# A macaron decoder block on one core: where the down stage's operands are combined, split and kept

## The chip, the cores and the metric

The kernel runs on one core of a Trainium2 chip. The metric is the time of one execution on the device, in microseconds; three runs of the kernel before the change stand at 2628.35, 2628.57 and 2629.67 us. The engines are TensorE (PE in the profile; PEld are its weight loads), VectorE (DVE), ScalarE (ACT) and GpSimd (POOL); SyncE (SP) issues most of the DMA transfers. Each engine works through its own instructions in order.

## The reference

The block is a half-step SwiGLU, a token mixer, a second half-step SwiGLU and a final RMS norm, on 1024 tokens of width 1024. The change touches only the two SwiGLU halves:

```python
D_MODEL, SEQ, D_FF = 1024, 1024, 2816

def swiglu(h, w_gate, w_up, w_down):
    return (jax.nn.silu(h @ w_gate) * (h @ w_up)) @ w_down

h = h + 0.5 * swiglu(rms_norm(h, ffn1_norm), ffn1_w_gate, ffn1_w_up, ffn1_w_down)
h = h + hybrid_mixer(rms_norm(h, mix_norm), ...)
h = h + 0.5 * swiglu(rms_norm(h, ffn2_norm), ffn2_w_gate, ffn2_w_up, ffn2_w_down)
return rms_norm(h, final_norm)
```

All of it is float32. The kernel reaches that precision with three matmuls for one: every operand x is split into hi (a cast to fp32r) and lo (x minus hi), and hi*lo, lo*hi and hi*hi are added up in PSUM.

## The kernel before, in words

Everything is kept transposed: 128 features on the partitions, 1024 tokens in the free dimension. D_FF is 22 tiles of 128 features, numbered j = 0 to 21.

**Gate/up stage** (`ffn`, `gate_up2`, `strassen`). Tiles 0 and 1 are made plainly, the others in pairs (j, j + 1), ten pairs in a half block. A pair is one Strassen run for the gate and one for up, each of seven products (`product`, twelve matmuls each, line 368) over sums of activation tiles that lie ready in SBUF (`t2`, `t3`, `t4` and `xs`). The weights come as four quarters a11, a12, a21, a22 in tiles `raw` (two buffers) and `sr` (two buffers); POOL makes the four sums of them that Strassen needs (`combine`, line 356), ACT casts the hi part (line 126) and DVE subtracts the lo part (line 127) for each product. ACT copies finished products out of PSUM (`keep`, line 374: c11 after the first product, c21 after the third, c22 after the fourth), DVE adds others to them (`add`, line 379). The third product is accumulated into the same PSUM bank as the first, after c11 is copied. The results of a pair are two tiles `s` of 1024 tokens, in halves: b11, b12 (the first tile), b21, b22 (the second). `put_gate` and `put_up` make silu(gate) * up in them; the last half to be ready is b12, from the seventh product of the up run. Both tiles of the pair are then stored to DRAM in float32 (`a_d`, line 490).

**Down stage.** First block D0 (tiles 18 and 19): `accumulate` with plain matmuls (line 139), update of h by DVE (line 282). Then four chunks of four tiles each (DCH), each a Strassen scheme over two parts (k = 0, 1) of two tiles: the part's seven operands b11, b21, t2, t3, t1, t4, b22 are made from its two tiles by four sums on POOL (lines 510, 511, 517 and 520, in `part_steps`) and seven splits (ACT line 126, DVE line 127). A chunk runs four groups g of seven products (`down`, line 575; 168 matmuls), each group with its weights loaded, summed on POOL (lines 586 to 589) and split; DVE adds each product into h (`put`, line 580). While a chunk runs, `prepare` loads the four float32 tiles of the next chunk from `a_d` (SP, line 548) and its operands are made, a step behind each weight split (`advance`). Chunk 0's first part is the pair just made (20, 21); its second part and the operands of its first part are made beside D0. The operands of even chunks lie in the tiles `t2h` to `t4l` and four smaller ones, those of odd chunks in the tiles that held the gate/up activations. The tail (tiles 12 to 15) is loaded and split at the end of the last chunk and runs with plain matmuls.

**What sets the order.** A scheduler of the framework sorts the instructions of each engine; what stands under `tc.high_priority` (weight splits, `keep`, `add`, `put`) goes ahead of its place in the program, and `tc.issue_after` holds an instruction behind a named one. On the chip an engine does not pass over an instruction that waits.

Of the kernel before, what the change touches and what calls it, by code (L numbers as in the profile page):

```python
# [7 lines left out]
F32 = mybir.dt.float32  # L8
F32R = mybir.dt.float32r
# [6 lines left out]
P = 128  # L16
T = 1024
# [3 lines left out]
NF = FF // P  # L21
# [2 lines left out]
NCH = T // P  # L24
QSQ = (EPS * P) ** 0.5
D0 = [18, 19]
DCH = [[20, 16, 21, 17], [0, 2, 1, 3], [4, 6, 5, 7], [8, 10, 9, 11]]
DTAIL = [12, 13, 14, 15]
HALVES = ((0, 512), (512, 512))
LO, HI = slice(0, 512), slice(512, 1024)  # L30
FIRST = ((0, 256), (256, 256), (512, 512))
# [17 lines left out]
def tile_macaron_hybrid(  # L49
# [123 lines left out]
    def run(steps):  # L173
        while True:
            try:
                next(steps)
            except StopIteration as e:
                return e.value
# [110 lines left out]
                for (ui, _, _), n in zip(units, ("t3h", "t3l", "t4h", "t4l"))]  # L289

    def s_tile(tp):
        return tp.tile([P, T], F32, name="s", tag="s", bufs=2)

    def norm_space(tp):
        w = [t[:, i * 512:i * 512 + 512] for t in (s_tile(tp), s_tile(tp)) for i in range(2)]
# [129 lines left out]
    def ffn(h, xs, wg, wu, wd, tq, tp, ysc, first, last, pre, steps, after):  # L425
        def act_tiles():
            return [tq.tile([P, T], F32R, name=n, tag=n, bufs=2) for n in ("ah", "al")]
# [20 lines left out]
            nc.sync.dma_start(out=a_d[j], in_=a)  # L448

        done = []  # L450
        a_d = dram.tile([NF, P, T], F32, name="a_d")

        def stage():
            return tp.tile([P, 512], F32, name="sr", tag="sr", bufs=2)
# [10 lines left out]
        def gate_up2(j):  # L465
            ss = [s_tile(tp), s_tile(tp)]

            def put_gate(i, sl, c, _):
                s, y = ss[i][:, sl], ysc[:, sl]
                with tc.high_priority(offset=400):  # L470
                    nc.vector.tensor_mul(out=s, in0=y, in1=c)
                    nc.scalar.activation(out=s, in_=s, func=AF.Silu)  # L472
                    nc.gpsimd.tensor_mul(out=s, in0=s, in1=y)  # L473

            strassen(wg[j], wg[j + 1], put_gate)
            hs = []

            def put_up(i, sl, c, _):
                s = ss[i][:, sl]
                with tc.high_priority(offset=400):  # L480
                    nc.vector.tensor_mul(out=s, in0=s, in1=c)
                    if j == D0[0]:
                        if not hs:
                            hs.extend(zip(act_tiles(), act_tiles()))
                        split(s, hs[0][i][:, sl], hs[1][i][:, sl])

            strassen(wu[j], wu[j + 1], put_up)
            if j < D0[0]:
                for i in (1, 0):
                    nc.sync.dma_start(out=a_d[j + i], in_=ss[i])  # L490
            return list(zip(*hs)) if hs else ss

        def part_steps(k, ss, ops):
            (b11, b12), (b21, b22) = ([t[:, LO], t[:, HI]] for t in ss)
# [30 lines left out]

        def chunk_ops(c):
            names = ("b11", "b21", "t2", "t3", "t1", "t4", "b22")
            res = {}
            for i, n in enumerate(names):
                if c % 2:  # L530
                    res[n] = [[t[:, k] for k in range(2)] for t in
                              (xn.tile([P, 2, 512], F32R, name=f"x{p}{i}", tag=f"x{p}{i}") for p in "hl")]
                elif i < 6:
                    m = ("t2h", "t2l", "t3h", "t3l", "t4h", "t4l")[i]
                    t = tq.tile([P, 4, 512], F32R, name=m, tag=m)
                    res[n] = [[t[:, 2 * p + k] for k in range(2)] for p in range(2)]
                else:
                    res[n] = [[tp.tile([P, 512], F32R, name=m, tag=m, bufs=bf) for m, bf in q]
                              for q in ((("c11", 1), ("c21", 1)), (("c22", 1), ("wt", 2)))]
            return res  # L540

        def prepare(c, ops, first=None):
            parts = [first] if first else []
            for k in range(len(parts), 2):
                ss = [p.tile([P, T], F32, name=n, tag=n, bufs=2)
                      for p, n in (((tq, "ah"), (tq, "al")) if k and c else ((tp, "s"), (tp, "s")))]
                for i in range(2):
                    nc.sync.dma_start(out=ss[i], in_=a_d[DCH[c][2 * i + k]])
                parts.append(ss)
            for k in range(2):  # L550
                yield from part_steps(k, parts[k], ops)
# [67 lines left out]
            gate_up2(j)  # L619
        acts = gate_up2(D0[0])  # L620
        ss = gate_up2(NF - 2)
        ops = chunk_ops(0)
        prep = prepare(0, ops, ss)
        advance(prep, None)
        accumulate(wd, block_units([D0])[0], acts, h, 0.5, step=lambda i: advance(prep, None))
        run(prep)
        for c in range(len(DCH)):
            prep = None
            if c + 1 < len(DCH):
                nops = chunk_ops(c + 1)  # L630
                prep = prepare(c + 1, nops)
                advance(prep, None)
            for g in range(4):
                down(wd[2 + 4 * c + g], ops, h[2 * g], h[2 * g + 1], prep)
            if prep:
                run(prep)
            ops = nops
        acts = []
        kept = []
        for n in ("t2h", "t2l"):  # L640
            t = tq.tile([P, 4, 512], F32R, name=n, tag=n).rearrange("p (j a) t -> p j (a t)", j=2)
            kept.append([t[:, k] for k in range(2)])
        for i, j in enumerate(DTAIL):
            t = s_tile(tp)
            nc.sync.dma_start(out=t, in_=a_d[j])
            acts.append([x[i] for x in kept] if i < 2 else act_tiles())
            split(t, *acts[-1])
        tail = [(2 + 4 * len(DCH) + i, 2 * i, 2) for i in range(4)]
        prev = (tail, acts)
        sqrt_table()  # L650
# [13 lines left out]
    with ExitStack() as st:  # L664
        tq = pool(st, "q1")
        hp = pool(st, "h1")
        tp = pool(st, "t1")
# [39 lines left out]
    with ExitStack() as st:  # L707
        with ExitStack() as stm:
            ys, h, tq = mixer(stm, st, tc, pool, start, xs2, load_unit, dense, ptile, bank, rsqrt_newton, split, new_x,
                           accumulate, block_units(OBLOCKS), dram, pr, ident, ones, cst, eye, wlr, win,  # L710
                           wout, y_d, h_d, sqrt_table, strassen_products, rp, psum, divide, recent, pinned, run)
        tp = pool(st, "t2")
# [10 lines left out]
        res = []  # L723
# [735 lines left out]
```

## Time and profile before

| | us |
|---|---|
| median of three runs | 2628.57 |
| the profiled execution, as a run | 2629.9 |
| its span in the trace | 2628.1 |
| gate/up stage, one pair | 38.08 |
| D0, first and second half block | 28.60, 26.89 |
| chunks 0 to 2 together, first and second half block | 134.31, 135.90 |
| chunk 3, first and second half block | 38.25, 38.80 |

The profile has one execution. Its span is the time from the first to the last instruction; the run's own time is a little longer. Stages are cut at the start of the first matmul that belongs to them. In a table of windows, the first number behind a stretch is its length, then follow the busy times of the engines with the number of instructions that begin in it, the clock granted to TensorE as a share of full speed, the busy share of the 16 DMA engines and the rate. A matmul's row gives its duration in the pipeline; consecutive matmuls start closer together than that.

### The profile page before, as it was taken

To read this page: it belongs to the slowest core of one execution; us is meant where nothing else is said; L and a number is where in the kernel's file an instruction comes from. 1 tells how busy PE (TensorE), PEld (TensorE's weight loads), DVE (VectorE), ACT (ScalarE), POOL (GpSimd) and SP (SyncE) were. 2 spreads that over 40 slices of the span, in tenths; PEclk is the share of its full clock that TensorE was granted. 3 is DMA by queue.
4 is the path that set the end of the run, shared out by engine and by line. 5 is a ranking of instruction groups with operands and counts; after the bars stand their busy time and mean duration, and the time that the engine had idled before them with its cause. 6 is when DMAs were issued, how large, how long until landed. Compare 5 with 4: busy or idle time off the path is not lost.

```text
span 2628.1 us, 32714 instructions
## 1 busy us (share of the span) xinstructions
PE 2490.9 (95%) x11656; PEld 2018.1 (77%) x11656; DVE 1877.5 (71%) x2907; ACT 1069.3 (41%) x1847; POOL 1175.8 (45%) x1312
## 2 busy tenths in 40 slices
PE   7899999899997999999989999999989999998998
PEld 6788888677866877777767787877868888886677
DVE  8855555899686778886686766767586555569996
ACT  5333334333252444443354544535243333343331
POOL 4554444654228667776351222122044444446631
PEclk9999999999998999999989999999989999999999
DMA  3222221322321222212211212113212222223222
GB/s 118 75 70 88 89 89 57 120 81 80 113 84 49 65 61 61 65 45 57 57 55 40 85 38 84 60 61 128 85 33 81 84 77 85 89 60 114 79 88 80
DMA packets 93602, 199.03 MB, mean 76 GB/s; under 512 B 12248, under 2 KB 17112, under 8 KB 93440
## 3 DMA queue, kind: packets, MB, share of 16 engines
q1 hardware_dynamic: 82576, 175.64, 20.6%
q0 software_dynamic: 8704, 18.89, 2.8%
q10 hardware_dynamic: 2160, 2.43, 0.3%
q8 instruction: 91, 1.49, 0.2%
q14 instruction: 71, 0.58, 0.1%
HBM read 158.73 MB, written 38.17 MB: 75 GB/s over the span
## 4 chain that ended last, share of the span: by engine, by line
PE 69%; DVE 14%; ACT 5%; issue 4%; POOL 3%; DMA 2%; DVEq 0%; POOLq 0%; ACTq 0%
PE q L368 28%; PE ps L139 15%; PE m L368 10%; PE q L575 6%; DVE wl L127 3%; PE q L989 2%; DVE h L580 1%; DVE xl L127 1%; DVE ha L580 1%; PE q L911 1%; DMA s<-a_d 1%; ACT L806 1%; PE q L1002 1%; PE q L1026 1%; POOL xp L936 1%
## 5 line engine op out<-in xcount | busy, mean ns | idle before, releaser
L127 DVE TENSOR_TENSOR wl<-raw,wh 128x512 fp32r<-128x512 f32 x244 | 209.3, 858 | 167.3 <-ACT wh L126 165.9
L139 PE MATMUL ps<-xl,wh 128*128 128x512 f32 (+2 forms) x736 | 257.1, 408 | 18.2 <-DVE xl L239 13.3
L127 DVE TENSOR_TENSOR wl<-sr,wh 128x512 fp32r<-128x512 f32 x232 | 204.0, 880 | 80.5 <-ACT wh L126 80.2
L139 PE MATMUL ps<-xh,wl 128*128 128x512 f32 (+2 forms) x736 | 254.4, 404 | 0.1
L139 PE MATMUL ps<-xh,wh 128*128 128x512 f32 (+2 forms) x736 | 254.0, 405 | 0.0
L368 PE MATMUL q<-xl,wh 128*128 128x512 f32 x640 | 249.0, 389 | 0.5 <-ACT c L374 0.5
L368 PE MATMUL q<-xh,wh 128*128 128x512 f32 x640 | 249.0, 389 | 0.0
L368 PE MATMUL q<-xh,wl 128*128 128x512 f32 x640 | 249.0, 389 | 0.0
L126 ACT CAST wh<-sr 128x512 fp32r<-128x512 f32 x232 | 143.8, 620 | 244.0 <-PE q L368 59.8
L473 POOL TENSOR_TENSOR s<-s,ysc 128x512 f32<-128x512 f32 x80 | 112.4, 1416 | 244.0 <-ACT s L472 244.0
L126 ACT CAST wh<-raw 128x512 fp32r<-128x512 f32 x244 | 144.7, 593 | 173.1 <-PE q L368 95.4
L139 PEld LDWEIGHTS ps<-xl,wh 128*128 128x128 f32 (+1 forms) x736 | 138.1, 192 | 49.5 <-DVE xl L239 8.7
L356 POOL TENSOR_TENSOR raw<-sr 128x512 f32<-128x512 f32 x20 | 27.3, 1367 | 331.3 <-DMA sr<-in_win 234.4
L139 PEld LDWEIGHTS ps<-xh,wl 128*128 128x128 f32 (+1 forms) x736 | 139.0, 192 | 24.2 <-issue 1.0
L139 PEld LDWEIGHTS ps<-xh,wh 128*128 128x128 f32 (+1 forms) x736 | 138.0, 192 | 24.5 <-issue 1.0
L368 PEld LDWEIGHTS q<-xl,wh 128*128 128x128 f32 x640 | 120.1, 188 | 25.8 <-issue 0.9
L368 PEld LDWEIGHTS q<-xh,wh 128*128 128x128 f32 x640 | 120.1, 188 | 25.0
L368 PEld LDWEIGHTS q<-xh,wl 128*128 128x128 f32 x640 | 120.1, 188 | 24.9
L379 DVE TENSOR_TENSOR c<-c,q 128x512 f32<-128x512 f32 x120 | 82.4, 687 | 74.6 <-PE q L368 74.5
L374 ACT COPY c<-q 128x512 f32<-128x512 f32 x120 | 70.6, 588 | 152.8 <-PE q L368 151.0
L933 POOL TENSOR_TENSOR itmp<-lt,xp 128x112 f32<-128x112 f32 (+29 forms) x248 | 114.6, 462 | 36.7 <-DMA lt<-l_d 17.9
L936 POOL TENSOR_TENSOR xp<-xp,itmp 128x112 f32<-128x112 f32 (+29 forms) x248 | 118.9, 480 | 19.4
(490 smaller groups left out, 6833.5 us busy)
## 6 DMA issues: line engine op xcount, KB each, us to landing
sr<-in_win SPq DMA_DIRECT2D x80, 256.0 KB, 2.6
a_d<-s SPq DMA_DIRECT2D x36, 512.0 KB, 3.7
raw<-in_win SPq DMA_DIRECT2D x66, 256.0 KB, 2.6
raw<-in_d SPq DMA_DIRECT2D x56, 256.0 KB, 2.6
raw<-in_g SPq DMA_DIRECT2D x48, 256.0 KB, 2.6
s<-a_d SPq DMA_DIRECT2D x24, 512.0 KB, 4.3
sr<-in_u SPq DMA_DIRECT2D x44, 256.0 KB, 2.9
raw<-in_u SPq DMA_DIRECT2D x44, 256.0 KB, 2.6
```

The lines of the kernel that those rows point to most:

```text
L126: a = nc.scalar.copy(out=hi, in_=src)
L127: b = (eng or nc.vector).tensor_sub(out=lo, in0=src, in1=hi.bitcast(F32))
L139: mm = nc.tensor.matmul(out=ps[:m, sl], lhsT=w[:, :m], rhs=x[:, sl], start=(i == 0 and a == 0), stop=(i == n - 1 and a == 2))
L368: nc.tensor.matmul(out=ps, lhsT=p[:, c], rhs=q, start=(first and k == 0 and a == 0), stop=(k == 3 and a == 2), skip_group_check=not first)
L374: marks[0] = nc.scalar.copy(out=t, in_=ps).ins
L379: marks[1] = nc.vector.tensor_add(out=t, in0=t, in1=ps).ins
L473: nc.gpsimd.tensor_mul(out=s, in0=s, in1=y)
L575: nc.tensor.matmul(out=ps, lhsT=p[:, c], rhs=q, start=(first and k == 0 and a == 0), stop=(k == 1 and a == 2), skip_group_check=not first)
L580: nc.vector.scalar_tensor_tensor(out=hd[:, sl], in0=ps, scalar=0.5, in1=hd[:, sl], op0=ALU.mult, op1=ALU.add)
L933: inv_eng.tensor_tensor(out=tv, in0=lp[:, j, j + 1:].unsqueeze(2).broadcast_to([P, r, m]), in1=xp[:, j, :m].unsqueeze(1).broadcast_to([P, ...
L936: inv_eng.tensor_tensor(out=xv, in0=xv, in1=tv, op=ALU.subtract)
L989: nc.tensor.matmul(out=q[:, c], lhsT=lhs[:, c], rhs=rhs[:, c], start=True, stop=True)
```

## The change

The operands of chunks 1 to 3 are no longer made in the down stage. As soon as a pair of the gate/up stage that belongs to one of these chunks is finished, `stage_part` makes its seven operands (four POOL sums, seven splits) and stores them as hi and lo to DRAM (`b_d`), eight stores a pair. The tail's pairs are split and stored the same way (`stage_tail`, `e_d`). In the down stage, `load_steps` issues the copies that bring the next chunk's operands (or the tail's) back, one behind each weight split, from POOL's queue. Chunk 0 now consists of the pair just made and of tiles 0 and 1, which are still stored in float32, so six of the ten pairs are staged and two are the tail's; the weights' order in DRAM follows. `s` has four buffers instead of two. In lines of the changed kernel: 128 and 129 are the casts and subtractions (126 and 127 before), 376 is the copy of c11 (374), 642 the update of h (580), 284 that of D0 (282).

```diff
-DCH = [[20, 16, 21, 17], [0, 2, 1, 3], [4, 6, 5, 7], [8, 10, 9, 11]]
+DCH = [[20, 0, 21, 1], [16, 2, 17, 3], [4, 6, 5, 7], [8, 10, 9, 11]]
+STAGED = {DCH[c][k]: (c, k) for c in range(1, len(DCH)) for k in range(2)}
+OPS = ("b22", "b11", "b21", "t3", "t1", "t2", "t4")
...
-        return tp.tile([P, T], F32, name="s", tag="s", bufs=2)
+        return tp.tile([P, T], F32, name="s", tag="s", bufs=4)
...
             if j < D0[0]:
-                for i in (1, 0):
-                    nc.sync.dma_start(out=a_d[j + i], in_=ss[i])
+                (stage_tail if j in DTAIL else stage_part)(j, ss)
...
+        def stage_part(j, ss):
+            c, k = STAGED[j]
+            (b11, b12), (b21, b22) = ([t[:, LO], t[:, HI]] for t in ss)
+            hl = []
+
+            def keep(n, b):
+                i = OPS.index(n)
+                if i % 2 == 0:
+                    hl[:] = act_tiles()
+                col = (i % 2) * 512
+                split(b, *(t[:, col:col + 512] for t in hl))
+                if i % 2 or i == 6:
+                    for p in range(2):
+                        nc.sync.dma_start(out=b_d[c][i - i % 2:i + 1, :, p, k, :].rearrange("n p t -> p n t"),
+                                          in_=hl[p].bitcast(F32)[:, :col + 512].rearrange("p (n t) -> p n t", t=512))
+
+            keep("b22", b22)
+            nc.gpsimd.tensor_sub(out=b22, in0=b22, in1=b12)
+            nc.gpsimd.tensor_sub(out=b12, in0=b12, in1=b11)
+            keep("b11", b11)
+            keep("b21", b21)
+            keep("t3", b22)
+            nc.gpsimd.tensor_add(out=b11, in0=b22, in1=b11)
+            keep("t1", b12)
+            nc.gpsimd.tensor_sub(out=b21, in0=b21, in1=b11)
+            keep("t2", b11)
+            keep("t4", b21)
...
+        def load_steps(fill):
+            pins = yield
+            for out, src in fill:
+                stack = ExitStack()
+                for p in pins or ():
+                    stack.enter_context(tc.issue_after(p))
+                with stack:
+                    nc.gpsimd.dma_start(out=out.bitcast(F32), in_=src)
+                pins = yield
...
         for c in range(len(DCH)):
-            prep = None
             if c + 1 < len(DCH):
-                nops = chunk_ops(c + 1)
-                prep = prepare(c + 1, nops)
-                advance(prep, None)
+                nops, fill = chunk_ops(c + 1)
+            else:
+                acts, fill = tail_acts()
+            prep = load_steps(fill)
+            advance(prep, None)
```

Three places in the order of instructions. First ACT, at the start of the gate product that follows a finished pair (here the second such place of the first half block). `raw`, `sr` and `wt` are weights, `ah` is a hi part of an operand or tile of the pair, `c_...<-q` is the copy of c11. Before:

```order
L126 CAST wh<-raw 128x512 x3
L126 CAST wh<-sr 128x512
L374 COPY c_1264<-q 128x512
L126 CAST wh<-wt 128x512
L126 CAST wh<-sr 128x512
```

and now:

```order
L128 CAST wh<-raw 128x512 x2
L128 CAST ah<-s 128x512
L128 CAST wh<-raw 128x512
L128 CAST ah<-s 128x512
L128 CAST wh<-sr 128x512
L128 CAST ah<-s 128x512 x3
L376 COPY c_1335<-q 128x512
L128 CAST wh<-wt 128x512
L128 CAST ah<-s 128x512
L128 CAST wh<-sr 128x512
```

The casts of b22 and b21 stand among the weight casts, those of t3, t1 and t2 ahead of the copy of c11, and that of t4 two instructions behind it.

Second DVE, in D0 of the first half block; `ha<-ps` are the updates of h, `t3l`, `t4h`, `t3h`, `t4l`, `t2h`, `t2l` and `wt<-s` are splits of chunk 0's operands, `wl` those of weights. Before:

```order
L127 TENSOR_TENSOR t3l<-s,t3l 128x512
L127 TENSOR_TENSOR t4h<-s,t4h 128x512
L282 SCALAR_TENSOR_TENSOR ha<-ps,ha 128x1024
L127 TENSOR_TENSOR t3h<-s,t3h 128x512
L127 TENSOR_TENSOR t4l<-s,t4l 128x512
L282 SCALAR_TENSOR_TENSOR ha<-ps,ha 128x1024 x2
L127 TENSOR_TENSOR t2h<-s,t2h 128x512
L127 TENSOR_TENSOR wl<-raw,wh 128x512
L127 TENSOR_TENSOR wt<-s,c_3620 128x512
L282 SCALAR_TENSOR_TENSOR ha<-ps,ha 128x1024
```

and now:

```order
L129 TENSOR_TENSOR t3l<-s,t3l 128x512
L284 SCALAR_TENSOR_TENSOR ha<-ps,ha 128x1024
L129 TENSOR_TENSOR t4h<-s,t4h 128x512
L129 TENSOR_TENSOR t3h<-s,t3h 128x512
L284 SCALAR_TENSOR_TENSOR ha<-ps,ha 128x1024
L129 TENSOR_TENSOR t4l<-s,t4l 128x512
L129 TENSOR_TENSOR t3l<-s,t3l 128x512
L129 TENSOR_TENSOR t4h<-s,t4h 128x512
L284 SCALAR_TENSOR_TENSOR ha<-ps,ha 128x1024
L129 TENSOR_TENSOR t3h<-s,t3h 128x512
```

Two splits of the second part, `t3l` and `t4h`, now stand ahead of the third update; before, the second part's first split came behind the third update.

Third DVE at the start of chunk 0; `ha<-q` are the updates of h, `xl_...<-s` splits of chunk 1's operands. Before:

```order
L580 SCALAR_TENSOR_TENSOR ha<-q,ha 128x512
L127 TENSOR_TENSOR xl_3812<-s,xh_3811 128x512
L580 SCALAR_TENSOR_TENSOR ha<-q,ha 128x512
L127 TENSOR_TENSOR wl<-raw,wh 128x512
L127 TENSOR_TENSOR xl_3800<-s,xh_3799 128x512
L580 SCALAR_TENSOR_TENSOR ha<-q,ha 128x512
L127 TENSOR_TENSOR xl_3802<-s,xh_3801 128x512
L580 SCALAR_TENSOR_TENSOR ha<-q,ha 128x512
L127 TENSOR_TENSOR wl<-wt,wh 128x512
```

and now:

```order
L642 SCALAR_TENSOR_TENSOR ha<-q,ha 128x512 x2
L129 TENSOR_TENSOR wl<-raw,wh 128x512
L642 SCALAR_TENSOR_TENSOR ha<-q,ha 128x512 x2
L129 TENSOR_TENSOR wl<-wt,wh 128x512
L642 SCALAR_TENSOR_TENSOR ha<-q,ha 128x512 x2
L129 TENSOR_TENSOR wl<-sr,wh 128x512
```

The splits of the next chunk's operands are gone; only updates and weight splits are left.

On SP, the eight stores of a staged pair stand ahead of three of the four weight loads of the next up product (before, two stores did); on POOL, the four sums of a pair stand behind the weight sums of the next gate product.

## Rows read from the trace of the kernel before

**Rows 1.** The page: its first line.
```profile
span 2628.1 us, 32714 instructions
```

**Rows 2.** Windows: busy us by engine (instructions), granted clock, DMA; pair, D0, chunks.
```profile
core 0: us, PE busy (x) PEld busy (x) DVE busy (x) ACT busy (x) POOL busy (x), PEclk, DMA share, GB/s
217.85:255.93 38.08, 38.08 (x170) 31.54 (x168) 21.05 (x29) 13.93 (x24) 17.32 (x12) 1.00 0.26 83
465.37:493.97 28.60, 24.56 (x97) 18.85 (x96) 23.30 (x23) 9.61 (x16) 19.36 (x15) 0.94 0.22 68
493.97:628.28 134.31, 121.21 (x505) 92.30 (x504) 128.93 (x177) 52.25 (x93) 79.70 (x71) 1.00 0.32 104
628.28:666.53 38.25, 38.25 (x169) 31.36 (x168) 32.44 (x51) 13.10 (x21) 8.96 (x11) 1.00 0.28 84
2365.28:2392.17 26.89, 23.05 (x97) 17.63 (x96) 23.32 (x23) 9.50 (x16) 19.38 (x15) 1.00 0.22 71
2392.17:2528.07 135.90, 122.81 (x505) 93.58 (x504) 128.78 (x177) 51.75 (x93) 79.98 (x71) 0.99 0.32 103
2528.07:2566.87 38.80, 38.58 (x169) 31.23 (x168) 32.43 (x51) 13.37 (x22) 8.79 (x11) 1.00 0.26 83
```

**Rows 3.** Waits of TensorE in both down stages: total us, times, longest.
```profile
PE q L575 <- DVE ha L580: 10.8, 14, 2.5
...
PE q L575 <- DVE h L580: 12.0, 16, 2.9
```

**Rows 4.** Lines: POOL's weight sums (mean ns); POOL-issued copies (ns, minimum, median, maximum).
```profile
L588 POOL TENSOR_TENSOR wt<-sr,raw 128x256 f32<-128x256 f32 x32 | 31.4, 981 | 1.9
...
L589 POOL TENSOR_TENSOR raw<-raw,wt 128x256 f32<-128x256 f32 x32 | 28.0, 875 | 78.6 <-DVE wl L127 78.6
...
L705 POOL DMA_DIRECT2D h_d<-ha x8: 531/572/728, 694.8 to 715.0; - x8
```

**Rows 5.** Timeline of TensorE: start, us, line, tiles, [idle before, releaser].
```profile
87.18 0.79 PE L368 MATMUL q<-t2l,wh 128*128 128x512 f32 x1 [6.61 <-ACT c L374]
```

**Rows 6.** Timeline of TensorE and ACT at a gate product's start.
```profile
234.42 0.62 ACT L126 CAST wh<-raw 128x512 fp32r<-128x512 f32 x1 [2.15 <-PE q L368]
...
236.89 0.39 PE L368 MATMUL q<-xl,wh 128*128 128x512 f32 x1
...
239.81 0.59 ACT L374 COPY c<-q 128x512 f32<-128x512 f32 x1 [2.10 <-PE q L368]
...
242.33 0.39 PE L368 MATMUL q<-t2l,wh 128*128 128x512 f32 x1
```

**Rows 7.** Timeline of TensorE, POOL and ACT at the down stage's start.
```profile
465.37 0.62 PE L139 MATMUL ps<-al,wh 128*128 128x512 f32 x2
...
466.47 1.61 POOL L510 TENSOR_TENSOR s<-s 128x512 f32<-128x512 f32 x1 [15.93 <-ACT wh L120]
...
469.86 1.61 POOL L517 TENSOR_TENSOR s<-s 128x512 f32<-128x512 f32 x1
...
471.50 0.62 ACT L126 CAST t3h<-s 128x512 fp32r<-128x512 f32 x1 [1.07 <-POOL s L517]
...
473.20 0.84 PE L139 MATMUL ps<-al,wh 128*128 128x512 f32 x2 [2.24 <-DVE ha L282]
```

**Rows 8.** Lines: POOL's three operand sums (mean ns).
```profile
L517 POOL TENSOR_TENSOR s<-s 128x512 f32<-128x512 f32 x10 | 15.9, 1589 | 1.9 <-DVE t2h L127 1.4
...
L511 POOL TENSOR_TENSOR s<-s 128x512 f32<-128x512 f32 x10 | 15.9, 1585 | 0.6
...
L510 POOL TENSOR_TENSOR s<-s 128x512 f32<-128x512 f32 x10 | 13.5, 1354 | 62.5 <-ACT wh L120 31.9 <-DVE xl L127 17.8 <-DVE wt L127 10.4
```

**Rows 9.** Timeline of POOL: weight sums in the gate/up stage.
```profile
231.25 1.30 POOL L356 TENSOR_TENSOR raw<-wt,raw 128x512 f32<-128x512 f32 x1 [0.70 <-DVE wl L127]
...
246.55 1.67 POOL L356 TENSOR_TENSOR wt<-sr 128x512 f32<-128x512 f32 x1
```

**Rows 10.** DMA issues: queue, count, KB each, median us to landing.
```profile
sr<-in_u SPq DMA_DIRECT2D x44, 256.0 KB, 2.9
```

More of the change, by code (lines that the diff above doesn't have):

```diff
@@ L450, in ffn @@
         done = []
-        a_d = dram.tile([NF, P, T], F32, name="a_d")
+        a_d = dram.tile([2, P, T], F32, name="a_d")
+        b_d = {c: dram.tile([7, P, 2, 2, 512], F32, name=f"b_d{c}") for c in range(1, len(DCH))}
+        e_d = {j: dram.tile([2, P, T], F32, name=f"e_d{j}") for j in DTAIL}
         def stage():
@@ L488, in gate_up2, with stage_tail @@
             if j < D0[0]:
-                for i in (1, 0):
-                    nc.sync.dma_start(out=a_d[j + i], in_=ss[i])
+                (stage_tail if j in DTAIL else stage_part)(j, ss)
             return list(zip(*hs)) if hs else ss
+        def stage_tail(j, ss):
+            for i, s in enumerate(ss):
+                hl = act_tiles()
+                split(s, *hl)
+                for p in range(2):
+                    nc.sync.dma_start(out=e_d[j + i][p], in_=hl[p].bitcast(F32))
+        def stage_part(j, ss):
[9 more added lines that the diff above has]
+                if i % 2 or i == 6:
+                    for p in range(2):
+                        nc.sync.dma_start(out=b_d[c][i - i % 2:i + 1, :, p, k, :].rearrange("n p t -> p n t"),
[11 more added lines that the diff above has]
+            keep("t4", b21)
         def part_steps(k, ss, ops):
@@ L527, in chunk_ops @@
             names = ("b11", "b21", "t2", "t3", "t1", "t4", "b22")
-            res = {}
+            res, fill = {}, []
             for i, n in enumerate(names):
+                src = b_d[c][OPS.index(n)] if c else None
                 if c % 2:
-                    res[n] = [[t[:, k] for k in range(2)] for t in
-                              (xn.tile([P, 2, 512], F32R, name=f"x{p}{i}", tag=f"x{p}{i}") for p in "hl")]
+                    ts = [xn.tile([P, 2, 512], F32R, name=f"x{p}{i}", tag=f"x{p}{i}") for p in "hl"]
+                    res[n] = [[t[:, k] for k in range(2)] for t in ts]
+                    fill += [(t, src[:, p]) for p, t in enumerate(ts)]
                 elif i < 6:
@@ L536, in chunk_ops @@
                     res[n] = [[t[:, 2 * p + k] for k in range(2)] for p in range(2)]
+                    if c:
+                        fill.append((t, src.rearrange("q p k t -> q (p k) t")))
                 else:
@@ L539, in chunk_ops, with tail_acts @@
                               for q in ((("c11", 1), ("c21", 1)), (("c22", 1), ("wt", 2)))]
-            return res
+                    if c:
+                        fill += [(res[n][p][k], src[:, p, k]) for p in range(2) for k in range(2)]
+            return res, fill
+        def load_steps(fill):
[7 more added lines that the diff above has]
+                pins = yield
+        def tail_acts():
+            kept, acts = [], []
+            for n in ("t2h", "t2l"):
+                t = tq.tile([P, 4, 512], F32R, name=n, tag=n).rearrange("p (j a) t -> p j (a t)", j=2)
+                kept.append([t[:, k] for k in range(2)])
+            for i in range(4):
+                acts.append([x[i] for x in kept] if i < 2 else act_tiles())
+            return acts, [(a[p], e_d[j][p]) for j, a in zip(DTAIL, acts) for p in range(2)]
         def prepare(c, ops, first=None):
@@ L544, in prepare @@
             for k in range(len(parts), 2):
-                ss = [p.tile([P, T], F32, name=n, tag=n, bufs=2)
-                      for p, n in (((tq, "ah"), (tq, "al")) if k and c else ((tp, "s"), (tp, "s")))]
+                ss = [s_tile(tp), s_tile(tp)]
                 for i in range(2):
@@ L621, in ffn @@
         ss = gate_up2(NF - 2)
-        ops = chunk_ops(0)
+        ops, _ = chunk_ops(0)
         prep = prepare(0, ops, ss)
@@ L627, in ffn @@
         for c in range(len(DCH)):
-            prep = None
             if c + 1 < len(DCH):
-                nops = chunk_ops(c + 1)
-                prep = prepare(c + 1, nops)
-                advance(prep, None)
+                nops, fill = chunk_ops(c + 1)
[3 more added lines that the diff above has]
+            advance(prep, None)
             for g in range(4):
                 down(wd[2 + 4 * c + g], ops, h[2 * g], h[2 * g + 1], prep)
-            if prep:
-                run(prep)
+            run(prep)
             ops = nops
[L638 to L647, printed above, removed]
         tail = [(2 + 4 * len(DCH) + i, 2 * i, 2) for i in range(4)]
```

## The prediction

> **What bounds the kernel now.** I read the stage table first, then who waits for whom inside a stage, then single instructions. The span is 2628.1 us [rows 1]; that execution took 2629.9 us, so 1.8 us lie around it, and it was 1.3 us above the median of 2628.57.
>
> In a gate/up pair TensorE sets the time: 38.08 us hold 168 matmuls, TensorE is busy in all of them, and VectorE (DVE), ScalarE (ACT) and GpSimd (POOL) are busy 21.05, 13.93 and 17.32 us [rows 2]. One matmul therefore takes 0.227 us, and one Strassen product (12 of them) 2.72 us. There is free time on the other engines, but none on TensorE.
>
> In the down stage VectorE sets it. A chunk is also 168 matmuls, 38.1 us. The first three chunks of the first half block take 134.31 us instead of 114.2, with VectorE busy 128.93 us (96%); those of the second take 135.90. The fourth chunk, beside which no operands of a next chunk are made, takes 38.25 and 38.80 us, with VectorE at 32.4 [rows 2]. The waits say the same: TensorE waits for the updates of h in line 580, and these stand behind operand splits on VectorE [rows 3].
>
> **The change, part by part.**
>
> *Chunks 0 to 2 lose their operand work.* Fourteen splits and eight POOL sums leave each of these chunks. What is left is the fourth chunk's work, so I take 38.5 us, the mean of its two times: 6 x 38.5 = 231.0 against 134.31 + 135.90 = 270.2. That is **-39.2**. What is late next is TensorE itself; the fourth chunk shows it never idle.
>
> *The loads that replace it* are issued by POOL: 14, 10, 14 and 8 of them in a half block. A POOL-issued copy of the same shape took POOL 0.53 to 0.73 us, median 0.57 [rows 4]. Chunk 0 thus gets 14 x 0.57 = 8.0 us more on POOL, beside 16 small weight sums of 0.88 to 0.98 us [rows 4], 15 us: 23 of 38 us. A load waits for the product that last read its tile, and the weight sums queue behind it; but POOL works about one group of weights (9.5 us) ahead. I put **+3** (0.5 us for each of six chunks); ends 0 and +10 (the third rival's price).
>
> *The same operands, made in the gate/up stage.* Each of six pairs per half block gets 7 casts on ACT, 7 subtractions on VectorE, 4 sums on POOL and 8 stores (two before). By busy time that fits: POOL 17.3 + 6.1 of 38.1 us, VectorE 21 + about 7. But the engines run in order, and one place does not fit. Operand t3 needs the first POOL sum, t1 the second, t2 the third. In the order, ACT's casts of t3, t1 and t2 stand ahead of the copy of c11 of the next gate product, and TensorE cannot begin that Strassen run's third product, which adds into the same bank, before c11 is copied. That TensorE does wait for this copy is seen once now: 6.61 us, at line 368 [rows 5].
>
> Today the next run's first product starts at 236.89, the copy runs from 239.81 for 0.59 us, and the third product starts at 242.33, 5.44 us after the first [rows 6]. How long the new chain is can be read from the down stage's start, where the same sums follow the same last product: TensorE moves on at 465.37, POOL starts the first sum at 466.47 (+1.10), the third at 469.86, and ACT casts its result at 471.50 (+6.13) [rows 7]. The copy would follow this cast (0.62), last 0.59 [rows 6, 7] and, by an estimate, release TensorE 0.1 us later: +7.4. The third product would be 2.0 us late. There all three sums took 1.6 us; by their mean durations, 1.354, 1.585 and 1.589 us [rows 8], with 0.08 between them as in rows 7, the third ends at 1.10 + 4.69 = +5.8 and TensorE starts at +7.1: 1.7 us late. With 1.30 us for each sum, POOL's shorter time [rows 9], it is 1.0. I take 1.7, since it rests on the means of exactly these three instructions. It happens after each of six staged pairs in both half blocks: 12 x 1.7 = **+20.4**; ends 12 x 1.0 = +12 and 12 x 2.0 = +24. The two tail pairs need no POOL sum: two long casts, done before the copy is due, so nothing.
>
> This wait is too short to cost clock as well, as far as the rows go: after a wait of 2.24 us at the down stage's start the next matmul pairs took 0.84 us instead of 0.62 [rows 7], and the granted clock of that stretch was 0.94, in the second half block 1.00 [rows 2]; the level falls, where it does, from 2.4 to 1.2 GHz.
>
> *The first block of the down stage (D0).* 96 matmuls, 21.8 us, take 28.60 and 26.89 us [rows 2]. Chunk 0's operands are still made here, but its second half now comes from pairs 0 and 1, stored long before, so its load leaves the chain and its sums follow at once on POOL. In VectorE's new order the third update of h stands behind a split of that second half, whose sum is POOL's sixth: 466.47 + 4 x 1.69 + 3 x 1.0 + 2 x 1.69, about 479.6, so the update ends near 482.5 while TensorE is ready at 478. One wait of about 4 us takes the place of three shorter ones, and the clock may fall behind it. I take +1 and +2, **+3** in all; ends -9 (VectorE's busy 23.3 us as the floor, twice) and +8.
>
> Nothing else on a path changes size; ACT also does one table load and the mixer's constants later, at the mixer's start, which I put at nothing.
>
> Sum: -39.2 + 3 + 20.4 + 3 = -12.8. Against the run's own 2629.9 that is 2617.1; carried to the median, 2628.57 - 12.8 = **2615.8, I say 2616**.
>
> **Rivals.**
>
> *The copy of c11 isn't late.* If POOL's sums start earlier than at the down stage, or take under 0.95 us each, the +20.4 goes: 2595. For it: ACT and VectorE have much free time. Against: all three casts stand ahead of the copy, and their chain begins only when the last product ends.
>
> *Slower than before: the stores hold up the weights.* SP issues the eight stores ahead of three of the four weight loads of the next up product. The last store waits for the last subtraction on VectorE, by the chain above about 11.7 us after the gate product starts, so the last load is issued near 12.6 and lands 2.9 us later [rows 10], at +15.5. Today the weight sums that wait for it start at 246.55 (+9.66) [rows 9]: 5.9 us earlier. Their third sum is ready 1.9 us before ACT's cast, which waits for TensorE anyway (232.55 and 234.42), and TensorE uses it at 242.33 [rows 6, 9]; less the four ACT instructions queued ahead of the copy, the sums can be late by 6.7 us, and 8.4 with the wait of 1.7. So 2.5 us are left. From a landing of 5.4 us on, each further microsecond costs 12; 2 us more give 2616 + 24 = 2640. For it: the stores are 3.5 MB per pair instead of 1, which at 83 GB/s and a DMA share of 0.26 [rows 2] makes some 149 GB/s and 0.47. Against: half of the DMA time stays free. It decides against the change from 2.5 + 12.8 / 12 = 3.6 us on top of a normal landing.
>
> *POOL sets the chunk.* VectorE is busy 32 of 38 us even in the fourth chunk. If each issue on POOL waits for two VectorE instructions (32.44 us / 51 = 0.64 us each [rows 2]), 14 issues take 14 x 1.85 = 26 us, with the sums 41: 2.4 us over, in the four chunks of the program with 14 loads (10 loads still fit). That is +10 in place of the +3: 2623. Against: the longest copy in rows 4 took 0.73. The Trainium skill, "DMA: Bandwidth & Descriptors", section "SWDGE vs HWDGE vs iDMA", says that GpSimd-issued copies keep their descriptor rings in SBUF state from which VectorE can lock GpSimd out, and that copies issued from SP are immune; by that rule this rival holds, and rows 4 do not bear it out.
>
> *The chunks don't get faster*, because something else than the splits holds them: 2628.6 + 20 + 3 = 2652. Against: the fourth chunk.
>
> **How the numbers follow.** Forecast 0.62 (2606 to 2624), no late copy 0.10 (2590 to 2603), POOL sets the chunk 0.11 (2617 to 2630), weights late 0.13 (2625 to 2660), chunks no faster 0.04. The range 2600 to 2630 leaves out most of the last two and half of the second. A measurement of this kernel tells about 0.2%, 5.3 us, from no change: faster means below 2623.3. That is nearly all of the first case, the second, half of the third: 0.72. Same: the rest of the third and a part of the fourth, 0.16. Slower: 0.12.
>
> **What would show it.** In the profile after: chunks 0 to 2 at 38 to 39 us, with no wait of line 580's successor on VectorE; twelve waits of 1.0 to 2.0 us of TensorE for ACT's c11 copy, 5.4 us into the gate product behind each staged pair, so pairs of 39.8 instead of 38.1 us; the weight sums of the next up product some 6 us later without TensorE waiting for them; one wait of about 4 us in D0. The prediction is wrong if TensorE waits in the gate/up stage for a weight load, if these waits exceed 2.2 us and the granted clock drops behind them, or if chunks stay at 44 us.

## The result, and the profile after

The changed kernel takes 2646.94 us (median of four runs, 2644.65 to 2651.4) against 2628.91 for the kernel before in the same series: the ratio is 1.0071, with a 95% interval of 1.0055 to 1.0087. It is 18 us slower; the prediction was 2616, 12.6 us below the 2628.57 from which it started. The profiled execution of after has a span of 2646.3 us against 2628.1 [rows 1], so its 18.2 us are what has to be explained.

| stage, cut at its first matmul | before | after | difference | forecast |
|---|---|---|---|---|
| up to the first gate/up product | 74.97 | 72.99 | -2.0 | 0 |
| gate/up, first half block | 390.40 | 421.48 | +31.1 | +10.2 |
| D0 | 28.60 | 31.76 | +3.2 | +1 |
| four chunks | 172.56 | 152.55 | -20.0 | -17.3 |
| tail, mixer, up to the second gate/up stage | 1317.95 | 1313.00 | -5.0 | 0 |
| gate/up, second half block | 380.80 | 409.78 | +29.0 | +10.2 |
| D0 | 26.89 | 29.86 | +3.0 | +2 |
| four chunks | 174.70 | 153.73 | -21.0 | -18.9 |
| tail | 61.23 | 61.15 | -0.1 | 0 |

The eight chunks gave 41 us, where 36 were forecast. The two gate/up stages took 60 us more, where 20 were forecast: these 40 us are more than the whole error of 31. The table of windows of after: a pair behind a staged one (207.58), a pair behind a tail pair (337.90; its first matmul starts at 337.95), D0, chunks 0 to 2, chunk 3, the second D0 (columns as in [rows 2]):

```profile
207.58:253.09 45.51, 40.31 (x170) 32.53 (x169) 31.70 (x38) 17.63 (x31) 23.98 (x16) 0.96 0.40 137
337.90:375.98 38.08, 38.08 (x169) 31.53 (x169) 25.61 (x31) 15.81 (x26) 16.87 (x12) 1.00 0.33 111
494.47:526.23 31.76, 25.46 (x98) 19.84 (x97) 24.34 (x24) 8.29 (x14) 20.72 (x20) 0.89 0.28 98
526.23:640.60 114.37, 114.37 (x506) 94.54 (x505) 87.93 (x133) 27.30 (x48) 55.09 (x83) 1.00 0.67 235
640.60:678.78 38.18, 38.18 (x169) 31.43 (x168) 30.13 (x48) 12.14 (x20) 9.74 (x13) 1.00 0.37 123
2401.56:2431.42 29.86, 24.09 (x97) 18.93 (x96) 23.67 (x23) 8.29 (x14) 21.47 (x20) 0.94 0.31 107
```

Chunks 0 to 2 of the first half block are 38.1 us each, TensorE is never idle in them, and VectorE's busy time is 87.93 us where it was 128.93 [rows 2]. The six pairs behind staged ones took 42.0, 43.2, 45.5, 41.5, 43.4 and 42.3 us in the first half block, the three others after the first pair 38.08. What TensorE waited for, in the first gate/up stage (behind its first pair) and in the second (total us, times, longest):

```profile
PE q L370 <- ACT c L376: 19.5, 10, 2.9
PE q L370 <- ACT c L376: 20.5, 11, 2.9
```

Only the copy of c11 appears, in 19 waits of 0.9 us and more: 12 in gate runs (29.9 us, as foreseen, but 2.5 us each instead of 1.7) and 7 in up runs (9.6 us), where none was forecast. The first gate run behind pair (6, 7) starts at 207.58. On POOL, ACT and TensorE (timeline of after: start, duration, line, tiles, [idle before, releaser]):

```profile
209.69 1.78 POOL L520 TENSOR_TENSOR s<-s 128x512 f32<-128x512 f32 x1 [3.09 <-ACT ah L128]
213.24 1.59 POOL L525 TENSOR_TENSOR s<-s 128x512 f32<-128x512 f32 x1
214.87 0.62 ACT L128 CAST ah<-s 128x512 fp32r<-128x512 f32 x1 [1.05 <-POOL s L525]
215.39 0.58 ACT L376 COPY c<-q 128x512 f32<-128x512 f32 x1
216.02 0.50 PE L370 MATMUL q<-t2l,wh 128*128 128x512 f32 x1 [2.84 <-ACT c L376]
```

This is the chain of the prediction: third sum on POOL, cast of t2, copy of c11, third product. But its first sum starts 2.1 us behind the product's start, not 1.1. The up run of the same pair, on SP (issues of the last store and of the weight loads behind it), POOL, ACT, VectorE and TensorE:

```profile
220.23 0.33 SPq L516 DMA_DIRECT2D b_d<-al  x1
220.61 0.42 SPq L354 DMA_DIRECT2D sr<-in_u  x1
221.94 0.33 SPq L354 DMA_DIRECT2D raw<-in_u  x1
222.32 0.42 SPq L354 DMA_DIRECT2D sr<-in_u  x1
227.84 1.29 POOL L358 TENSOR_TENSOR wt<-sr 128x512 f32<-128x512 f32 x1 [6.49 <-DVE s L475]
230.58 1.29 POOL L358 TENSOR_TENSOR raw<-wt,raw 128x512 f32<-128x512 f32 x1
231.90 0.62 ACT L128 CAST wh<-raw 128x512 fp32r<-128x512 f32 x1 [3.49 <-POOL raw L358]
232.56 1.23 DVE L129 TENSOR_TENSOR wl<-raw,wh 128x512 fp32r<-128x512 f32 x1 [4.21 <-ACT wh L128]
233.71 1.78 DVE L475 TENSOR_TENSOR s<-ysc,c 128x512 f32<-128x512 f32 x1
235.52 0.63 ACT L476 ACTIVATE s<-s 128x512 f32<-128x512 f32 x1 [3.00 <-DVE s L475]
237.10 0.56 ACT L376 COPY c<-q 128x512 f32<-128x512 f32 x1
237.71 0.50 PE L370 MATMUL q<-t2l,wh 128*128 128x512 f32 x1 [2.35 <-ACT c L376]
```

Counted from the gate run's start, the last weight load is issued at +14.7 us, behind the eighth store (+12.65), and takes about 5.4 us to land, where 2.9 was usual [rows 10]. This is the longest such landing; behind the other staged pairs of this half block the last load left at +13.7 to +15.3 and took 3.1 to 3.6 us. POOL's sums start at +20.3 instead of about +9.7 [rows 9]. The row names VectorE's line 475 as the end of POOL's wait, but this sum reads only loaded weights, and behind all six staged pairs of this half block it starts 0.13 us after the last load has landed.

The third sum ends at 231.87. ACT's cast of it follows, then VectorE's subtraction, which waits for the cast, and behind it on VectorE the product of line 475; ACT's silu waits 3.0 us for that product, and the copy of c11 stands behind the silu, one more cast and one more silu. TensorE starts 5.84 us after the sum and waits under the copy's name. In all seven up runs that wait 0.9 us or more this distance is 5.84 to 5.86 us.

So two mechanisms stood side by side in the trace: **A**, the staged casts ahead of the copy of c11 (forecast), and **B**, the stores ahead of the weight loads (the slower rival, chance 0.13).

### The profile page after: what moved, and what is told of

Read it like the earlier page. It is cut to its first block, busy times and chain, and to the rows that moved or that the text cites. A ratio compares the mean times of both kernels' runs of the same rounds, so it can differ in the third digit from the quotient of the medians.

```text
span 2646.3 us, 32939 instructions
## 1 busy us (share of the span) xinstructions
PE 2490.4 (94%) x11656; PEld 2028.9 (77%) x11656; DVE 1945.8 (74%) x2907; ACT 1064.3 (40%) x1845; POOL 1224.6 (46%) x1404
## 4 chain that ended last, share of the span: by engine, by line
PE 69%; DVE 14%; ACT 6%; POOL 5%; issue 4%; DMA 3%; SPq 0%; POOLq 0%; ACTq 0%; DVEq 0%
PE q L370 21%; PE ps L141 17%; PE q L637 11%; PE m L370 10%; PE q L1041 2%; DVE wl L129 2%; DVE al L129 1%; DMA raw<-in_g 1%; PE q L963 1%; ACT ah L128 1%; POOL s L520 1%; DVE c L381 1%; POOL s L521 1%; ACT wh L128 1%; DVE s L485 1%
## 5 line engine op out<-in xcount | busy, mean ns | idle before, releaser
L129 DVE TENSOR_TENSOR wl<-raw,wh 128x512 fp32r<-128x512 f32 x244 | 215.6, 884 | 149.8 <-ACT wh L128 144.6
L129 DVE TENSOR_TENSOR wl<-sr,wh 128x512 fp32r<-128x512 f32 x232 | 215.9, 931 | 77.1 <-ACT wh L128 77.0
L477 POOL TENSOR_TENSOR s<-s,ysc 128x512 f32<-128x512 f32 x80 | 121.4, 1527 | 147.8 <-ACT s L476 147.8
L358 POOL TENSOR_TENSOR wt<-sr 128x512 f32<-128x512 f32 x40 | 59.4, 1484 | 155.2 <-DMA sr<-in_g 82.2
L129 DVE TENSOR_TENSOR al<-s,ah 128x512 fp32r<-128x512 f32 (+1 forms) x100 | 108.4, 1087 | 27.2 <-ACT ah L128 21.1
L370 PE MATMUL m<-xl,wh 128*128 128x512 f32 x320 | 127.2, 397 | 0.1
```

The lines of the kernel that those rows point to most:

```text
L358: nc.gpsimd.tensor_tensor(out=o, in0=a, in1=b, op=op)
L370: nc.tensor.matmul(out=ps, lhsT=p[:, c], rhs=q, start=(first and k == 0 and a == 0), stop=(k == 3 and a == 2), skip_group_check=not first)
```

## Experiments

Before each run the theories were A, B, C (the traffic of the stores slows the stage, no order matters), D (order of h's updates in D0) and E (the four buffers of `s`). A ratio is to the kernel before in the same series; its median there lay between 2627.0 and 2630.0 us, so times of different series compare to about 3 us.

### A alone: casts behind c11

```diff
-            keep("t3", b22)  ...  keep("t4", b21)
+            # in the next pair's gate run, behind the copy of c11:
+            with tc.issue_after(marks[0]):
+                keep("t3", b22); keep("t1", b12); keep("t2", b11); keep("t4", b21)
```

> Only the place of ACT's casts of t3, t1, t2 and t4 changes: they are held behind the copy of c11 of the next gate product. Theory A (order on ACT: the copy of c11 waits behind casts whose POOL sums are late): the twelve waits of TensorE for this copy in the gate runs behind staged pairs, 14.9 and 15.0 us in the changed kernel, go. The cast of the fourth product's weights now stands behind the same three casts, so up to 1 us may stay at each of the twelve. Theory B (stores on SP hold up the weight loads of the up run, and the copy of c11 of the up run comes late through ACT's queue) is not touched: waits of 9.6 us in the up runs stay or grow a little. By A and B about 2646.9 - 30 - 10 (clock) + 6 = 2613, between 2600 and 2625. Theory C (the stores' traffic, not any order, slows the stage): the same waits under another name, 2640 to 2650.

2632.33 us (1.0026, 1.0017 to 1.0035): 14.6 us less, 13.2 of them in the two gate/up stages (414.78 and 403.27). That is less than half of the 34 expected, and the time lies in the range of neither theory. The waits of the first gate/up stage behind its first pair:

```profile
PE q L370 <- ACT c L376: 17.5, 12, 2.7
```

None of them is for c11 in a gate run any more. Six (8.6 us) have moved two products on, to the copy of c21 at +11.9 to +12.8 us: 1.4 us each, not under 1. In the gate run that starts at 206.02 a staged cast and a silu stand ahead of that copy, and the silu waited 2.9 us for VectorE, where its input stood behind two staged subtractions (3.5 us). The waits in the up runs have become six with 9.0 us, from three with 4.3: the last store left about 1 us later (+13.6 instead of +12.6), the last weight load at about the same time, and TensorE, held up less in the gate run, came to the up run 0.8 to 2.9 us sooner. A is right about the gate runs' waits for c11, and B about the direction in which its own waits moved.

### B alone: stores of four pairs left out

```diff
-                if i % 2 or i == 6:
+                if (i % 2 or i == 6) and c == 1:
...
-                src = b_d[c][OPS.index(n)] if c else None
+                src = b_d[1][OPS.index(n)] if c else None
```

> Left out: the stores of the staged operands of tiles 4 to 11 (four of six pairs per half block); the loads of all chunks read what pairs 2 and 16 stored, so the result is not the reference's. Casts, subtractions and sums stay. Theory A: the gate-run waits for the copy of c11 stay at 2.8 us behind all six pairs (15 to 17 us per half block). Theory B: the up-run waits (0.9 to 2.4 us) behind these four pairs go, since the up weights are loaded as in the kernel before; total 2646.9 - 9 and some clock, 2630 to 2642. Theory C (traffic of the stores): gate waits go as well, pairs of 38.1 behind the four, 2605 to 2612.

2629.94 us (1.0013, 1.0003 to 1.0022). The waits of the first stage behind the four pairs without stores, all in gate runs:

```profile
PE q L370 <- ACT c L376: 8.6, 4, 2.7
```

There is no wait in an up run behind these pairs, in either half block; behind the two that still store there is one in three of four cases (0.96, 1.44, 1.25 us). In the gate runs the waits stay: 1.8 to 2.2 us, apart from the first of the four (2.7 and 3.0 us), whose pair still ran beside the stores of the one before. The gate run that starts at 205.95, with nothing late from before (POOL, ACT, TensorE):

```profile
207.01 1.79 POOL L520 TENSOR_TENSOR s<-s 128x512 f32<-128x512 f32 x1 [3.09 <-ACT ah L128]
212.22 0.62 ACT L128 CAST ah<-s 128x512 fp32r<-128x512 f32 x1 [1.06 <-POOL s L525]
212.74 0.58 ACT L376 COPY c<-q 128x512 f32<-128x512 f32 x1
213.37 0.50 PE L370 MATMUL q<-t2l,wh 128*128 128x512 f32 x1 [1.82 <-ACT c L376]
```

POOL at +1.06, the cast at +6.27, TensorE at +7.42: the prediction read +1.10, +6.13 and +7.4 off [rows 7] and then took +7.1. So A alone is nearly of the size that was forecast, and the further 0.6 to 1.0 us of the changed kernel's gate waits go with the stores: with them a late up run ends with VectorE and ACT about 1 us behind TensorE (the next to last product of line 485 on VectorE starts 0.68 us behind the gate run's start at 207.58, and here 0.36 us ahead of it). C falls for the gate runs: their waits stayed without the traffic. For the up runs this kernel cannot tell B from C, since the traffic went with the stores; the next one can. The two gate/up stages are 19.2 us shorter (410.86 and 401.21) with 8 of 12 pairs' stores gone; for all twelve that makes, by an estimate, 29 us for the stores. The remaining 60.1 - 1.7 (first pair) - 29 = 29 us would be A's, waits and what follows them. No run moves the stores alone, so this split stays an estimate.

### Both: casts behind c22

The same edit as for A, but at the mark of c22's copy, 11 us into the gate run. The scheduler then also puts the later six stores behind all four weight loads of the up run.

> The four casts are held behind the copy of c22 of the next gate run, some 11 us into it; by this the later six of the eight stores also come behind all four weight loads of the up run. Theories A and B together: no wait of TensorE for ACT in the gate/up stages apart from the first pair's, every pair 38.08 us, no loss of clock there: gate/up 392 and 381 us instead of 421.5 and 409.8, 2646.9 - 59 = 2588 (2583 to 2597). A alone (B wrong, the up-run waits come from elsewhere): 2597 to 2605. Theory C (traffic): the same bytes are stored, so 2635 to 2650.

**2597.73 us** (0.9896, 0.9877 to 0.9914): faster than both kernels, with the same bytes stored, so C falls for the up runs too. In the gate run that starts at 199.19 the last weight load leaves at +11.4 us, ahead of six of the eight stores:

```profile
210.59 0.33 SPq L354 DMA_DIRECT2D raw<-in_u  x1
211.92 0.38 SPq L523 DMA_DIRECT2D b_d<-ah  x1
```

No wait for ACT is left in either stage behind the first pair; the one that is new is VectorE's add of c22, behind two subtractions of staged operands:

```profile
PE q L370 <- DVE c L381: 4.2, 6, 0.9
PE q L370 <- DVE c L381: 4.3, 6, 0.8
```

The gate/up stages take 398.18 and 386.96 us. The expectation of 2588 (at most 2597) left out this wait, 12 times about 1 us; by time alone 2597.7 lies in the window of "A alone", and it is the missing waits in the up runs that decide.

### The order in D0

```diff
+            # second part only: t1, t2, t4 behind the 3rd, 4th, 5th update of h
+            with tc.issue_after(updates[2]):
                 keep("t1", b12)
```

> In the first block of the down stage (D0) the last three splits of the second part are held behind the third, fourth and fifth update of h on VectorE. Theory D (the order on VectorE: the third update stands behind a split whose sum is POOL's sixth): the wait of 4.07 us shrinks to about 1.3 us and the low clock behind it goes; D0 31.8 and 29.9 us become 27 to 29, chunk 0 stays at 38.1; 2646.9 - 6 = 2641 (2637 to 2644). Rival (VectorE or POOL has too much work in D0, the order only says where the wait shows): D0 stays within 1 us or chunk 0 gets longer by what D0 loses, 2645 to 2649.

2645.55 us (1.0076, 1.0061 to 1.0091), no difference that this series can tell from 2646.94, and in the rival's range. The trace shows part of it: D0 takes 29.33 and 28.60 us instead of 31.76 and 29.86, and the chunks of a half block are 0.2 and 0.6 us longer. TensorE's waits in the first D0, of after and of this kernel:

```profile
PE ps L141 <- DVE ha L284: 6.3, 3, 4.1
PE ps L141 <- DVE ha L287: 5.1, 4, 2.4
```

So the order on VectorE makes 1.7 us of the longest wait of 4.07, and 1.2 of 6.3 us in all. That the rest is work is not shown alone: the kernel below with D0 at 25 us has half of the splits and sums and a new order as well.

### Four buffers of `s` in the kernel before

```diff
-        return tp.tile([P, T], F32, name="s", tag="s", bufs=2)
+        return tp.tile([P, T], F32, name="s", tag="s", bufs=4)
```

> The kernel before with four buffers of the tile s instead of two, and nothing else of the change. Theory E: these buffers move the prologue's and the mixer's start (norm space, the tables and constants of the mixer), and that is where the changed kernel's 5.0 us less between the first tail and the second gate/up stage, its 2.0 us less ahead of the first gate/up stage and its 1.7 us more in the first pair come from: span between these cuts 1312 to 1314 instead of 1318, first product stall 8.3 instead of 6.6 us, total 2621 to 2625. Rival: they come with the other parts of the change (staging, loads) or are scatter between executions: stages as before, 2626 to 2629.

2620.49 us (0.9972, 0.9961 to 0.9984). The stretch from the first tail to the second gate/up stage, 1317.95 us before and 1313.00 after, is here

```profile
662.40:1976.58 1314.18, 1242.50 (x6138) 1002.76 (x6137) 947.53 (x1652) 578.62 (x995) 571.59 (x845) 0.98 0.22 66
```

and the first product waits 8.3 us instead of 6.6 [rows 5], the stage ahead being 3.7 us shorter. E holds for most of it: 3.8 of the 5.0 us there, and the gain ahead of the first gate/up stage, are the buffers' doing; each of these stretches is read from one trace. That the chunks also took 2.8 and 3.5 us less here, and D0 0.6 and 2.3 more, was not expected, and why is open.

### Further: spread casts, chunk 0 staged too

Four more kernels tried for what was left in the best one. First the staged splits were spread over the two runs, then D0's order was added:

> As the kernel with the casts behind c22, but the four staged splits are also held behind VectorE's updates of the gate run, two at a time, and the last ones go into the up run. There, each pair behind a staged one still took 39.0 to 39.3 us, with a wait of 0.6 to 0.9 us for VectorE's add of c22, which stood behind two long subtractions (3.5 us). Theory (order on VectorE): these waits go, pairs of 38.1, gate/up 391.5 and 381, total 2597.7 - 12 = 2586 (2584 to 2590). Rival (VectorE has no room for them anywhere): the wait shows elsewhere, 2594 to 2600.

> The former kernel with the D0 order of the earlier run as well (last three splits of the second part behind the third to fifth update of h): D0 from about 30 and 31 to 28.5 us each, 4 us less than the former kernel: about 2582. Rival: D0's gain is lost again in chunk 0 or in the stage before, 2585 to 2588.

2598.93 us (0.9889, 0.9872 to 0.9905): the add of c22 is no longer waited for, but four waits of some 0.5 us for ACT have come (2.2 us in all) and four of the six pairs behind staged ones still take 39.3 to 39.6 us (the other two 38.1 and 38.4): the rival was right. With D0's order **2594.93 us** (0.9870, 0.9855 to 0.9884), the lowest of all, 4.0 us less, which is the forecast difference, though not its level of 2582; D0 takes 29.39 and 28.59 us, at a granted clock of 1.00 in the first:

```profile
469.18:498.57 29.39, 22.98 (x98) 17.71 (x96) 24.09 (x23) 8.30 (x14) 21.10 (x20) 1.00 0.32 106
```

Then chunk 0's second part was staged as well, in three places:

> The kernel with spread splits, and chunk 0's second part (tiles 0 and 1) is staged as well, in the first pair's runs, stored as hi and lo and loaded by eight POOL copies at the start of D0; D0 then makes one part's operands instead of two: seven splits and four sums less. Theory D' (D0 is set by the splits and sums that stand among the updates of h): D0 from 30 to 22 to 25 us (floor 21.8, its 96 matmuls), total about 2586 - 13 = 2573 (2569 to 2578). Rival (the eight loads, 3.5 MB, land too late for chunk 0, or the pair behind the first one waits): chunk 0 longer by 3 to 8 us, 2578 to 2586.

> Chunk 0's second part staged once more, with the two places mended that the former run showed: in the first pair the staged casts are held behind c22 of the up run instead of the gate run (there TensorE waited 7.8 and 6.6 us for the copy of c11), and in D0 the four sums of the remaining part go ahead of chunk 0's weight sums on POOL and its last splits behind the updates of h on VectorE (there TensorE waited 7.2 and 7.7 us for an update). Theory: D0 from 29.4 and 28.6 us to 23 to 26, the first pair back at 49.4 and 38.1 (up to 1.3 more each), one more staged pair 1.3 us; total 2594.9 - 8 = 2587 (2583 to 2591). Rival (the eight loads at the start of D0 delay the weights, whatever the order): D0 28 or more, 2593 to 2605.

> D0 as in the former run (25.3 and 24.4 us), but tiles 0 and 1 are stored in float32 as before and loaded back beside the pair of tiles 14 and 15, where no other pair is staged; their casts are held behind c22 of its gate and of its up run. In the former run the two sets of casts met in the second pair, which took 46.6 and 45.1 us instead of 38.3. Theory: that pair is back at 38.3, the pairs of tiles 14 to 17 take 38.1 to 39.4, total 2597.9 - 8.3 - 6.9 + 2 = 2585 (2581 to 2589). Rival (a seventh staged pair costs its time wherever it stands): the lost 7 us turn up at tiles 14 to 17, 2593 to 2599.

The first took 2620.17 us (0.9967), far from both expectations (2569 to 2586): mechanism A again, a wait of 7.8 us for c11 in the first pair, and in D0 one of 7.2 us, since the sums queued on POOL behind a weight sum whose load was late. The second took 2597.87 (0.9886) instead of 2583 to 2591: D0 fell as forecast,

```profile
476.32:501.66 25.34, 22.59 (x98) 17.79 (x96) 18.09 (x20) 6.01 (x10) 15.63 (x18) 1.00 0.59 213
2356.56:2380.94 24.38, 22.62 (x97) 17.77 (x96) 18.52 (x20) 6.02 (x10) 15.66 (x18) 1.00 0.58 208
```

but the second pair rose to 46.62 and 45.06 us, with a wait of 4.9 us for c11. The third took 2599.75 (0.9893) instead of 2581 to 2589: the pairs of tiles 14 to 17 rose by 4.6 and 1.8 us in the first half block and by 2.6 and 2.8 in the second, and D0 was 26.60 and 25.96. In these two a seventh staged pair cost at least what it saved, as the rival of the third run had it.

## Why the prediction was wrong, step by step

- **Chunks, -39.2 and +3 for the loads: right, and 4.8 us better.** -41.0 together. The chunks took 38.1 us in the first half block and 38.4 on average in the second, so the loads cost next to nothing; each of POOL's copies took 0.53 to 0.72 us, as in [rows 4]. The rival "POOL sets the chunk" did not come. The rule of the Trainium skill ("DMA: Bandwidth & Descriptors", section "SWDGE vs HWDGE vs iDMA") that VectorE, while it is in a two-port mode, locks GpSimd out of the memory in which it writes the descriptors of its copies did not show either, with VectorE busy 77% of chunks 0 to 2. No run here shows in which mode VectorE ran, so the rival did not follow from the rule alone.
- **The copy of c11, +20.4: mechanism right, twelve waits right, size nearly right where nothing else is late.** 1.7 us each were forecast; 1.8 to 2.2 were measured behind pairs without stores, and 2.5 on average with them.
- **"This wait is too short to cost clock": wrong.** In this trace it held for waits under 2 us; in three other runs a wait of 1.8 or 1.9 us was followed by 7 or 8 slow matmuls. Of the ten waits of 2.2 us and more in the two stages, seven were followed by 7 or 8 matmuls that started 0.43 us apart instead of 0.227, some 1.5 us each; and the first matmuls behind any wait cost about 0.3 us more. By the starts of matmuls, the 60 us of the gate/up stages are 41 of waits, 11 of slow matmuls and 7 of restarts; 1 is not placed. The rows I leaned on [rows 7] had one wait of 2.24 us.
- **The step that failed: the 2.5 us of slack in the slower rival, because of which the sum put the late weight loads at nothing.** The rival's first parts were nearly right: the last load forecast near +12.6 left at +13.7 to +15.3, and landed 3.1 to 3.6 us later, once 5.4. What was mis-sized is the stretch from the third weight sum to TensorE. The prediction counted four ACT instructions there, which leaves 9.8 - 6.7 = 3.1 us; in all seven up runs with a wait it was 5.84 to 5.86, because ACT's silu waited 3.0 us for VectorE, whose product stood behind the subtraction of the same late weights. These 2.7 us are more than the whole slack. In the pair that starts at 253.09 the load left at +13.65 and landed 3.2 us later, 1.4 us later than forecast and inside the stated slack, and TensorE still waited 1.04 us. (The prediction also took the sum at +9.66 for one that waits for the last load; in the trace of before that load left at +10.2, and it is the third sum, at +13.4, that needs it.)
- **The sign that was looked for was too narrow.** "TensorE waits for a weight load" was to show the rival, while ACT and VectorE, working in order, carried the lateness to the copy of c11. Another of the signs did come: waits above 2.2 us with a fall of the granted clock behind them. And both mechanisms lengthened one another, where the prediction only added their prices: with the stores the gate waits were mostly 2.8 us, without them 1.8 to 2.2. The stores are worth about 29 us by the estimate above; the rival's 24 were an example for 2 us past its slack, and its range of 2625 to 2660 holds the measured 2647.
- **D0, +3: 6.1.** The forecast's one wait of about 4 us came (4.07, and the granted clock of that stretch fell to 0.89), but the first of the old waits, 2.24 [rows 7], stayed too with 1.7. In the run with four buffers of `s` alone D0 was 0.6 and 2.3 us longer as well, so how much of the 6.1 is the new order's stays open.
- **"Nothing else on a path changes size": wrong by -7.0 and, in the first pair, +1.7**, by the run with these alone mostly from the buffers of `s`, which I had read only as space for the pairs.

Forecast -12.8; measured -41.0 + 60.1 + 6.1 - 7.0 = +18.2.

## What to carry to other kernels

Work that is moved to where engines have free time brings its place in each engine's order with it: look for what is queued behind each moved cast, and behind each store on the queue that also loads the weights. When such work must go in, hold it behind the copies that TensorE needs, and its stores behind the loads; here the casts held behind the next copy alone gave 2632 us, held behind a later one, with six of the stores behind the weight loads, 2598, for the same work as in 2647. When a forecast leans on slack, follow the late work to TensorE through every engine that hands it on: each hand-over can add a wait. And two delays that pass through the same engine are not simply added: each can lengthen the other.

## What was not expected of the hardware

A wait of TensorE of one and the same length costs clock or doesn't. After 2.83 us at 172.81 the granted clock of the next 4.19 us was 0.61, with seven matmuls 0.43 us apart, the lower of the two levels (1.2 of 2.4 GHz); after 2.84 us at 216.02 it stayed at 1.00 (windows of after, columns as above). What makes the difference, no run here shows:

```profile
172.81:177.00 4.19, 4.19 (x12) 3.31 (x13) 4.13 (x6) 2.23 (x4) 0.97 (x2) 0.61 0.81 314
216.02:220.00 3.98, 3.98 (x17) 3.30 (x18) 3.94 (x6) 2.58 (x5) 0.76 (x2) 1.00 0.85 329
```

A subtraction on VectorE of 128x512 took 0.68 to 0.70 us while POOL was idle (61 of them in the first gate/up stage behind its first pair), and 0.7 to 1.8, median 1.4, where POOL was at work when it started (89). This makes the staged splits dearer than their count, since they follow POOL's sums (timeline of after: one alone, one and then three beside the staged sums):

```profile
207.66 0.68 DVE L129 TENSOR_TENSOR wl<-raw,wh 128x512 fp32r<-128x512 f32 x1
210.24 1.77 DVE L129 TENSOR_TENSOR wl<-sr,wh 128x512 fp32r<-128x512 f32 x1
212.15 4.92 DVE L129 TENSOR_TENSOR al<-s,ah 128x512 fp32r<-128x512 f32 x3
```
